# The convolution's last rows: from one turn a tile to one turn for each group of tiles

## The chip, the cores and the metric

The program runs on one core of one Trainium2 chip. The time is the device time of one execution in microseconds; of several runs the median counts. One more execution was profiled, and the profile's times are those of that execution. The granted TensorE clock was 1.00 in it throughout.

A core has five engines that work side by side, each with an instruction queue of its own that it takes strictly in order: PE (TensorE: matmuls and transposes, into PSUM banks), DVE (VectorE), ACT (ScalarE), POOL (GpSimd) and SP (SyncE, which here only issues transfers). PEld is TensorE's loading of the stationary operand. ACT issues transfers as well; while its queue does that, the instructions behind the issue wait.

## What is computed

One step of a hybrid decoder layer, for a prompt of 512 tokens and for 8 sample sequences of 8 tokens each, all in 32-bit floats. The part that matters is the causal depthwise convolution over 3072 channels (x: 2048, B: 512, C: 512), which also returns the last three rows of its input for each sequence:

```python
def causal_conv(xbc, conv_prev, conv_w, conv_b):
    L = xbc.shape[1]
    xa = jnp.concatenate([conv_prev.astype(xbc.dtype), xbc], axis=1)
    y = conv_b + sum(xa[:, j:j + L] * conv_w[j] for j in range(D_CONV))
    return jax.nn.silu(y), xa[:, L:]
```

`xbc` is a slice of `rms(h) @ W_in`. The second result goes to the outputs `conv_p` (3 rows of 3072 channels) and `conv_s` (8 sequences, 3 rows each). Around this stand a first feed-forward block, attention with a paged cache, a chunked state-space scan over 4 groups of heads that uses the convolution's result, projections, and a second feed-forward block.

## The kernel before

Activations lie transposed: channels on the 128 partitions, the 576 tokens (512 of the prompt, then 64 of the samples) along the free dimension. Matrices are multiplied in three passes: weights and activations are split into a rounded upper part and a remainder, and `mm3` (L207 to L217) adds upper by upper, upper by lower and lower by upper. It works on a half of 288 tokens at a time; for 1024 input channels a half is 8 x 3 = 24 matmuls into one PSUM bank. `acc()` hands out that bank; here it has two of them (tag "acc"). `split` (L170 to L178) makes the two parts of a weight tile: ACT the upper one (L176), DVE or, every second time, POOL the lower one (L177). Each part has four buffers, and a convolution tile takes two of each.

`conv_tile` computes one tile of 128 channels. POOL clears three columns before the prompt (L1184) and copies the samples' previous rows in (L1185); two halves of matmuls follow; DVE evicts the first (L1189), the second's prompt part (L1194) and its samples (L1196) into the tile `xr`, which is 3 + 512 + 8 x 11 columns wide. Then the last columns of `xr`, 91 of them (three of the prompt, eleven for each sample sequence), are turned on TensorE (L1202) into columns 384 to 511 of the very bank that held the second half, ACT copies the turned rows to the tile `tt` (L1204), and four transfers on ACT's queue store them: one for `conv_p` (L1205) and three for `conv_s` (L1208), one for each of the three rows. The convolution itself is one ACT instruction (L1213), three on DVE (L1215), a tanh on ACT that overwrites `xr` (L1216), and the products on DVE (L1217), ACT (L1219) and POOL (L1220).

`group_in(g)` calls `conv_tile` six times for a group: for B, for C, and for four tiles of x; there are 4 groups, so 24 tiles. `group_scan(g)` (L1295 on) is the scan of a group. Its `chunk` turns the x tiles and B with transposes (L1370, L1377, copied by ACT at L1380) and multiplies (L1386, L1390), `carry` passes the state on (L1401, L1407), and POOL scales (L1364, L1311). These small products live in banks that `sm()` hands out, two of them (tag "mm"). In the program's text the next group's `group_in` comes after a group's scan, and the scan after the `group_in` that feeds it.

The order of each engine's queue is not the order of the text. A planner simulates the time line of all engines while the program is built; it takes what is ready, the first in the text first, and what stands under `soon()` ahead of the rest. It also lets a tile of a ring (`bufs=2` and the like) wait until the readers of an earlier tile in the same buffer are done. Rings that matter here: `xr` three buffers, `tt` one, `acc` two banks, `sm()` two banks.

In time, the first group's convolutions run at 875 to 912 us, beside the end of the attention; the other groups' lie among the scan before them, at 961 to 1034, 1100 to 1142 and 1192 to 1246 us.

Of the kernel before, what the change touches and what calls it, by code (L numbers as in the profile page):

```python
# [17 lines left out]
AF = mybir.ActivationFunctionType  # L18
# [5 lines left out]
P = 128  # L24
OFFSET = 3000
D = 1024
NP = 512
NS = 64
NT = NP + NS
HT = NT // 2  # L30
B = 8
T = 8
# [3 lines left out]
CONV = 3072  # L36
# [6 lines left out]
CZ, CX, CB, CC, CDT = 0, 2048, 4096, 4608, 5120  # L43
# [46 lines left out]
def ap3(ap, offset, dims):  # L90
    return bass.AP(tensor=ap.tensor, offset=ap.offset + offset, ap=[list(d) for d in dims])


def build(ctx, tc, A, O):
    nc = tc.nc
    uid = [0]

    def tl(pool, shape, dt=F32, tag=None, bufs=None):
        uid[0] += 1
        kw = {} if bufs is None else {"bufs": bufs}  # L100
        return pool.tile(shape, dt, tag=tag, name=f"{tag}_{uid[0]}", **kw)
# [5 lines left out]
    act = nc.scalar.activation  # L107
    V = nc.vector
    G = nc.gpsimd

    constp = ctx.enter_context(pool("const"))
# [10 lines left out]
    ident = tl(constp, [P, P], tag="ident")  # L122
# [12 lines left out]
    def sm():  # L135
        return bank("mm", 2)
# [6 lines left out]
    def acc(full=False):  # L143

        wide[1] += 1
        a = wide[0]() if wide[0] and wide[1] % 2 else tl(accp, [P, 512], tag="acc")
        return a if full else a[:, :HT]
# [275 lines left out]
    with pool("h1", reuse_waits="tile") as hp:  # L423
        hts = [tl(hp, [P, NT], tag=f"h{k}") for k in range(8)]
        nrm1 = Norm(0)
        with pool("xin", side="right", reuse_waits="tile") as xi:
# [4 lines left out]
            for half in range(2):  # L431
                d = slice(half * (D // 2), (half + 1) * (D // 2))
                for c in range(5):
                    n = P if c < 4 else NS
# [5 lines left out]
            t = tr()  # L440
            nc.tensor.transpose(t[:, :8], r1, ident[:8, :8])
            V.tensor_copy(P1[:, :8], t[:, :8])
            for k in range(8):
                t = tr()
# [6 lines left out]
                t = sm()  # L451
# [5 lines left out]
            for c in range(5):  # L457
                n = P if c < 4 else NS
# [6 lines left out]
        with pool("setup2", side="right", reuse_waits="tile") as su:  # L465
            q = nc.scalar

            r1 = tl(su, [66, P], tag="r1")

            def rows(o, ap, n):  # L470
                q.dma_start(out=r1[o:o + n, :], in_=ap.rearrange("o (k p) -> (o k) p", p=P))

            rows(0, A["ffn1_norm"], 8)
            rows(8, A["mix_norm"], 8)
            rows(16, A["ffn2_norm"], 8)
            rows(24, A["ssd_norm"], 16)
            rows(40, A["conv_b"], 24)
            for i in range(2):
                q.dma_start(out=r1[64:65, i * 64:(i + 1) * 64], in_=A["q_norm"])
                q.dma_start(out=r1[65:66, i * 64:(i + 1) * 64], in_=A["k_norm"])  # L480
            t = tr()
            nc.tensor.transpose(t[:, :66], r1, ident[:66, :66])
            V.tensor_copy(P1[:, 8:], t[:, 8:66])
            V.tensor_scalar(P1[:, 40:64], t[:, 40:64], 0.5, None, ALU.mult)
            V.tensor_scalar(P1[:, 64:65], t[:, 64:65], -0.125, None, ALU.mult)
            r2 = tl(su, [96, P], tag="r2")
            q.dma_start(out=r2, in_=A["conv_w"].rearrange("o j (k p) -> (o j k) p", p=P))
            P2 = tl(constp, [P, 96], tag="P2")
            t = tr()
            nc.tensor.transpose(t[:, :96], r2, ident[:96, :96])  # L490
            V.tensor_scalar(P2, t[:, :96], 0.5, None, ALU.mult)
            r3 = tl(su, [16, 2], tag="r3")
            q.dma_start(out=r3, in_=A["d_skip"].rearrange("o (j e) -> (o j) e", e=2))
            r4 = tl(su, [16, 2, 64], tag="r4")
            V.tensor_copy(r4, r3.unsqueeze(2).to_broadcast([16, 2, 64]))
            dsk = tl(constp, [P, 16], tag="dsk")
            t = tr()
            nc.tensor.transpose(t[:, :16], r4.rearrange("j e p -> j (e p)"), ident[:16, :16])
            V.tensor_copy(dsk, t[:, :16])

            bb = tl(constp, [48, 1], tag="bb")
            behind(q.dma_start(out=bb[:32], in_=A["dt_bias"].rearrange("o h -> h o")), nrm1.insts[7])
            behind(q.dma_start(out=bb[32:48], in_=A["b_f"].rearrange("o h -> h o")), nrm1.insts[7])
            V.tensor_scalar(bb[32:48], bb[32:48], -1.0, None, ALU.mult)
            al = tl(constp, [48, 1], tag="al")
            V.memset(al, 0.0)
            behind(q.dma_start(out=al[:32], in_=A["a_log"].rearrange("o h -> h o")), nrm1.insts[7])
            act(al, al, AF.Exp)
            V.tensor_scalar(al, al, -1.0, None, ALU.mult)

            pcol = tl(su, [P, B], I32, tag="pcol")
            for b in range(B):
                q.dma_start(out=pcol[:, b:b + 1], in_=ap3(A["page_table"], b * NPG, [(1, NPG), (0, 8), (1, 1)]))
            rq = tl(su, [P, 4], tag="rq")
            q.dma_start(out=rq, in_=A["consts"][:, COFF["rq"][0]:COFF["rq"][0] + 4])
            pidx = tl(constp, [P, B, 4], I32, tag="pidx")
            pf32 = tl(su, [P, B], tag="pf32")
            V.tensor_copy(pf32, pcol)
            V.tensor_scalar(pf32, pf32, 32.0, None, ALU.mult)
            V.tensor_tensor(pidx, pf32.unsqueeze(2).to_broadcast([P, B, 4]), rq.unsqueeze(1).to_broadcast([P, B, 4]), ALU.add)  # L520
# [67 lines left out]
    win = A["w_in"][0]  # L588
# [18 lines left out]
    with pool("dtf", side="right", reuse_waits="tile") as dp:  # L607
        w = []
# [7 lines left out]
        for half in range(2):  # L616
            a = pv()
# [29 lines left out]
        for c in range(5):  # L647
            n = P if c < 4 else NS
            t = tr()
# [17 lines left out]
    with pool("att", side="right", reuse_waits="tile") as ap:  # L667
# [95 lines left out]
        for p in range(2):  # L763
            for g2 in range(0, 4, 2):
# [9 lines left out]
                for gi in range(2):  # L774
                    w = []
# [8 lines left out]
        for p in range(2):  # L784
            t = tl(mixp, [P, NT], tag="kf", bufs=2)
# [390 lines left out]

    XR = [P, 3 + NP + B * (T + 3)]

    def conv_tile(ct, w, prev, out):

        xr = tl(xz, XR, tag="xr", bufs=3)
        xsamp = xr[:, 3 + NP:]
        xsamp = xsamp.rearrange("p (b u) -> p b u", u=T + 3)
        G.memset(xr[:, :3], 0.0)  # L1184
        first = G.tensor_copy(xsamp[:, :, :3], prev.rearrange("p (j b) -> p b j", b=B))  # L1185
        a = acc()
        mm3(a, w, xs, 0)
        with soon():
            V.tensor_tensor(xr[:, 3:3 + HT], a, rbc[:, hs(0)], ALU.mult)  # L1189
        a = acc(True)  # L1190
        full, a = a, a[:, :HT]
        end = mm3(a, w, xs, 1)
        with soon():
            V.tensor_tensor(xr[:, 3 + HT:3 + NP], a[:, :NP - HT], rbc[:, HT:NP], ALU.mult)  # L1194
        with soon():
            V.tensor_tensor(xsamp[:, :, 3:], a[:, NP - HT:].rearrange("p (b t) -> p b t", t=T),  # L1196
                            rbc[:, NP:].rearrange("p (b t) -> p b t", t=T), ALU.mult)

        n = 3 + (T + 3) * B
        with soon():  # L1200
            t = full[:n, 512 - P:]
            nc.tensor.transpose(t, xr[:, NP:], ident)  # L1202
            tt = tl(xz, [n, P], tag="tt", bufs=1)
            act(tt, t, AF.Copy)  # L1204
        nc.scalar.dma_start(out=O["conv_p"][0, 0, :, ct * P:(ct + 1) * P], in_=tt[:3])  # L1205
        for j in range(3):
            r = 3 + T + j
            nc.scalar.dma_start(out=O["conv_s"][0, :, j, ct * P:(ct + 1) * P], in_=tt[r:r + (T + 3) * (B - 1) + 1:T + 3])  # L1208

        m = NP + B * (T + 3)  # L1210
        cv = tl(mixp, XR, tag="kf", bufs=2)
        wc = lambda j: P2[:, j * 24 + ct:j * 24 + ct + 1]
        act(cv[:, :m], xr[:, :m], AF.Identity, bias=P1[:, 40 + ct:41 + ct], scale=wc(0))  # L1213
        for j in range(1, 4):
            V.scalar_tensor_tensor(cv[:, :m], xr[:, j:j + m], wc(j), cv[:, :m], ALU.mult, ALU.add)  # L1215
        tanh = act(xr[:, :m], cv[:, :m], AF.Tanh)  # L1216
        last = V.scalar_tensor_tensor(out[:, :NP], xr[:, :NP], 1.0, cv[:, :NP], ALU.add, ALU.mult)  # L1217
        samples = lambda v: v[:, NP + 3:].rearrange("p (b u) -> p b u", u=T + 3)[:, :, :T]
        act(samples(xr), samples(xr), AF.Identity, bias=1.0)  # L1219
        G.tensor_tensor(out[:, NP:].rearrange("p (b t) -> p b t", t=T), samples(xr), samples(cv), ALU.mult)  # L1220
        convs.append((first, tanh, last, end))
# [3 lines left out]
    def group_in(g):  # L1225

        scT = tl(xz, [P, 6, 24], tag="scT", bufs=1)
        nc.sync.dma_start(out=scT[:, :4, :], in_=scD[:, 4 * g:4 * g + 4, :])
        nc.sync.dma_start(out=scT[:, 4:, :], in_=ap3(scD, (16 + g) * 24, [scD.ap[0], (4 * 24, 2), (1, 24)]))
        bT = tl(xz, [P, NT], tag="bT", bufs=2)  # L1230
        conv_tile(16 + g, Cols(win, CB + g * P, width=P).get(0), scT[:, 4, :], bT)
        cT = tl(xz, [P, NT], tag="cT", bufs=2)
        conv_tile(20 + g, Cols(win, CC + g * P, width=P).get(0), scT[:, 5, :], cT)
        xc = Cols(win, CX + g * 512)
        xg = tl(xz, [P, 4, NT], tag="xg", bufs=2)
        for i in range(4):
            conv_tile(4 * g + i, xc.get(i), scT[:, i, :], xg[:, i, :])
        return bT, cT, xg

    nxt = group_in(0)  # L1240
# [346 lines left out]
```

## Time and profile before

| | |
|---|---|
| median of 3 runs | 1829.32 us (1826.55 to 1835.17) |
| the profiled execution | 1829.29 us |
| its span, first to last instruction | 1827.4 us |
| turns L1202 | 24, 0.272 us each |
| copies L1204 | 24, 0.273 us each |
| transfer issues L1205, L1208 | 24 of 0.256 us, 72 of 0.651 us |

The page's first lines give each engine's busy time, its share of the span and its number of instructions. Matmuls are pipelined: one lasts 0.29 us in the trace while the next starts 0.13 us after it, so a busy share of 98% of PE does not say that it starts a matmul whenever it could. In the view of waits a row names who waited, whose end released it, the total in us, the number of times and the longest. In the timeline a row has start, duration, engine, line, operation, what is written and read, and in brackets the idle time of the engine before it with its releaser. In the rows of one line stand minimum, median and maximum in ns. A row of the windows has the stretch, its length, the busy time and number of instructions of each engine, the granted clock, the share of the DMA engines and GB/s.

### The profile page before, as it was taken

What the parts mean: (1) busy time and instruction counts of PE and PEld (TensorE: products, weight loads), DVE (VectorE), ACT (ScalarE), POOL (GpSimd) and SP (SyncE); (2) the same over time, 40 slices, a digit from 0 to 9 for tenths busy, and PEclk for the clock granted to TensorE, in tenths of its full rate; (3) what the DMA queues carried; (4) which work ended last, traced back from release to release, by engine and by line L of the source; (5) the groups of instructions that cost most, each with busy time, mean ns of one, the idle gap of its engine ahead of it and who ended that gap; (6) DMA issues with size and microseconds to landing.
All of it is one profiled execution on the core that took longest, in us unless ns stands there. A gap on an engine that the chain in (4) does not pass through costs nothing.

```text
span 1827.4 us, 38776 instructions
## 1 busy us (share of the span) xinstructions
PE 1798.5 (98%) x15315; PEld 1713.3 (94%) x15315; DVE 1014.7 (56%) x2259; ACT 758.1 (41%) x1598; POOL 630.6 (35%) x724
## 2 busy tenths in 40 slices
PE   8999999999999999999999999999999999999999
PEld 7999999999999888888998888888999999999998
DVE  4643334434426777775728857686675444444542
ACT  4333223334324565564427555555333333123322
POOL 0433002312322455453325454848452322002210
PEclk9999999999999999999999999999999999999999
DMA  5544443444546688774356554454473434543342
GB/s 164 161 120 138 129 134 109 124 137 133 120 132 197 201 243 240 244 231 158 89 164 183 153 139 112 124 151 138 153 215 93 127 116 130 152 139 110 111 124 66
DMA packets 297739, 269.72 MB, mean 148 GB/s; under 512 B 55084, under 2 KB 262108, under 8 KB 297404
## 3 DMA queue, kind: packets, MB, share of 16 engines
q1 hardware_dynamic: 229712, 184.16, 35.7%
q10 hardware_dynamic: 57844, 46.10, 8.2%
q0 software_dynamic: 10000, 36.97, 6.4%
q8 instruction: 121, 1.98, 0.5%
q14 instruction: 62, 0.51, 0.1%
HBM read 223.72 MB, written 38.73 MB: 144 GB/s over the span
## 4 chain that ended last, share of the span: by engine, by line
PE 88%; DVE 5%; DMA 3%; ACT 1%; issue 1%; POOL 1%; ACTq 0%; DVEq 0%; SPq 0%; POOLq 0%
PE acc L212 17%; PE acc L215 16%; PE acc L216 16%; PE pv L212 8%; PE pv L215 8%; PE pv L216 8%; PE tr L990 2%; PE tr L977 1%; PE mm L913 1%; PE pv L1386 1%; PE pv L944 1%; PE mm L931 1%; DVE kf L1215 1%; PE mm L1401 1%; PE pv L1028 1%
## 5 line engine op out<-in xcount | busy, mean ns | idle before, releaser
L176 ACT ACTIVATE whi<-stage 128x512 fp32r<-128x512 f32 (+2 forms) x474 | 294.3, 622 | 687.2 <-PE acc L215 589.1
L212 PE MATMUL acc<-xh,whi 128*128 128x288 f32 x1792 | 539.4, 301 | 11.1 <-DVE xr L1189 4.8
L215 PE MATMUL acc<-xl,whi 128*128 128x288 f32 x1792 | 530.4, 296 | 0.0
L216 PE MATMUL acc<-xh,wlo 128*128 128x288 f32 x1792 | 529.3, 295 | 0.0
L177 DVE TENSOR_TENSOR wlo<-stage,whi 128x512 fp32r<-128x512 f32 (+1 forms) x373 | 262.3, 703 | 257.1 <-ACT whi L176 235.0
L212 PEld LDWEIGHTS acc<-xh,whi 128*128 128x128 f32 x1792 | 336.4, 188 | 17.7 <-DVE xr L1189 7.2
L215 PEld LDWEIGHTS acc<-xl,whi 128*128 128x128 f32 x1792 | 336.6, 188 | 1.3 <-issue 1.2
L216 PEld LDWEIGHTS acc<-xh,wlo 128*128 128x128 f32 x1792 | 336.2, 188 | 0.9 <-issue 0.7
L353 POOL TENSOR_TENSOR u<-u,s 128x288 f32<-128x288 f32 x88 | 82.3, 936 | 433.9 <-DVE u L352 378.2
L177 POOL TENSOR_TENSOR wlo<-stage,whi 128x512 fp32r<-128x512 f32 (+1 forms) x101 | 133.9, 1326 | 276.3 <-ACT whi L176 243.3
L212 PE MATMUL pv<-xh,whi 128*128 128x288 f32 (+1 forms) x720 | 213.3, 297 | 0.6 <-ACT xh L227 0.6
L215 PE MATMUL pv<-xl,whi 128*128 128x288 f32 (+1 forms) x720 | 211.7, 294 | 0.0
L216 PE MATMUL pv<-xh,wlo 128*128 128x288 f32 (+1 forms) x720 | 211.6, 294 | 0.0
L212 PEld LDWEIGHTS pv<-xh,whi 128*128 128x128 f32 (+1 forms) x720 | 134.2, 186 | 1.2 <-ACT xh L227 0.8
L215 PEld LDWEIGHTS pv<-xl,whi 128*128 128x128 f32 (+1 forms) x720 | 134.1, 186 | 1.2
L216 PEld LDWEIGHTS pv<-xh,wlo 128*128 128x128 f32 (+1 forms) x720 | 134.0, 186 | 0.2
L212 PE MATMUL pv<-hh,whi 128*128 128x288 f32 x352 | 105.7, 300 | 0.0
L215 PE MATMUL acc<-hl,whi 128*128 128x288 f32 x352 | 104.1, 296 | 0.0
L212 PE MATMUL acc<-hh,whi 128*128 128x288 f32 x352 | 104.1, 296 | 0.0
L215 PE MATMUL pv<-hl,whi 128*128 128x288 f32 x352 | 104.1, 296 | 0.0
L216 PE MATMUL acc<-hh,wlo 128*128 128x288 f32 x352 | 104.1, 296 | 0.0
L216 PE MATMUL pv<-hh,wlo 128*128 128x288 f32 x352 | 103.7, 295 | 0.0
(370 smaller groups left out, 3560.1 us busy)
## 6 DMA issues: line engine op xcount, KB each, us to landing
stage<-in_w_in_dram SPq DMA_DIRECT2D x52, 512.0 KB
stage<-in_ffn_w_up_dram SPq DMA_DIRECT2D x44, 512.0 KB
stage<-in_ffn_w_gate_dram SPq DMA_DIRECT2D x43, 512.0 KB
stage<-in_ffn_w_down_dram SPq DMA_DIRECT2D x40, 512.0 KB
h<-in_state_ssm_dram SPq DMA_DIRECT2D x64, 256.0 KB
hTD<-hT ACTq DMA_DIRECT2D x32, 256.0 KB
pb<-pastD SPq DMA_DIRECT2D x32, 256.0 KB
ab<-cumD SPq DMA_DIRECT2D x32, 256.0 KB
```

The lines of the kernel that those rows point to most:

```text
L176: act(hi, view, AF.Copy)
L177: e.tensor_tensor(lo, view, hi.bitcast(F32), ALU.subtract)
L212: begin = mm(out, lhsT=hi, rhs=a, start=first and i == 0, stop=False)
L215: mm(out, lhsT=hi, rhs=b, start=False, stop=False)
L216: end = mm(out, lhsT=lo, rhs=a, start=False, stop=last and i == n - 1)
L353: G.tensor_tensor(u, u, sil[half], ALU.mult)
L913: mm(s[:, :n], lhsT=q, rhs=ks[2 * self.p + e][:, :n], start=hl == 0, stop=hl == 1)
L931: nc.tensor.transpose(t[:, j * P:(j + 1) * P], lt[:, j * P:(j + 1) * P], ident)
L944: mm(self.ob[o:o + 32, i * P:(i + 1) * P], lhsT=vtok[j][:, v0:v0 + 32], rhs=self.pts[e][:, j * P:(j + 1) * P], start=j == 0, stop=j == i)
L977: nc.tensor.transpose(t[:, i * P:(i + 1) * P], kk[:, i, p * P:(p + 1) * P], ident)
L990: mm(s[kv * 32:(kv + 1) * 32, :], lhsT=self.q(kv), rhs=self.kT[kv // 2], start=True, stop=True)
L1028: mm(ob[kv * 32:(kv + 1) * 32, :64], lhsT=self.pt[:, i * P + kv * 32:i * P + (kv + 1) * 32], rhs=vv[:, i, kv * 64:(kv + 1) * 64], start=jq ...
```

## The change

The last rows are no longer turned tile by tile. A tile `tail` of 27 columns for each convolution tile gathers them: POOL copies the three last columns of the prompt and the 8 x 3 last columns of the samples out of `xr` (two copies a tile, under `soon()`). Columns are ordered so that after the turn the prompt's rows of all tiles come first and the samples' after them. `store3`, called once for B and C together and once for the four x tiles, turns the whole of it in a bank of `sm()`, copies it once on ACT and stores it with two transfers on ACT's queue. These are 8 turns, 8 copies and 16 transfers in place of 24, 24 and 96, and 48 new copies on POOL. `tail` and `tt` have one buffer each. `store3` is not under `soon()`. Besides, two constants of one column each, `bb` and `al`, become the columns of one tile.

```diff
-            bb = tl(constp, [48, 1], tag="bb")
+            ba = tl(constp, [48, 2], tag="ba")
+            bb, al = ba[:, :1], ba[:, 1:]
...
-            al = tl(constp, [48, 1], tag="al")
...
+    def rows3(n):
+
+        return tl(xz, [P, 108], tag="tail", bufs=1)[:, :27 * n]
+
+    def store3(tail, n, ct, step):
+
+        t = sm()
+        nc.tensor.transpose(t[:27 * n, :P], tail, ident)
+        tt = tl(xz, [108, P], tag="tt", bufs=1)
+        act(tt[:27 * n], t[:27 * n, :P], AF.Copy)
+        for name, r0, rows in (("conv_p", 0, 3), ("conv_s", 3 * n, 24)):
+            nc.scalar.dma_start(out=ap3(O[name], ct * P, [(step * P, n), (CONV, rows), (1, P)]), in_=tt[r0:r0 + rows * n])
+
-    def conv_tile(ct, w, prev, out):
+    def conv_tile(ct, w, prev, out, last3):
...
-        a = acc(True)
-        full, a = a, a[:, :HT]
+        a = acc()
...
-        n = 3 + (T + 3) * B
+        tail, i, n = last3
         with soon():
-            t = full[:n, 512 - P:]
-            nc.tensor.transpose(t, xr[:, NP:], ident)
-            tt = tl(xz, [n, P], tag="tt", bufs=1)
-            act(tt, t, AF.Copy)
-        nc.scalar.dma_start(out=O["conv_p"][0, 0, :, ct * P:(ct + 1) * P], in_=tt[:3])
-        for j in range(3):
-            r = 3 + T + j
-            nc.scalar.dma_start(out=O["conv_s"][0, :, j, ct * P:(ct + 1) * P], in_=tt[r:r + (T + 3) * (B - 1) + 1:T + 3])
+            G.tensor_copy(tail[:, 3 * i:3 * i + 3], xr[:, NP:NP + 3])
+            G.tensor_copy(tail[:, 3 * n + 24 * i:3 * n + 24 * (i + 1)].rearrange("p (b j) -> p b j", j=3), xsamp[:, :, T:])
...
+        tail = rows3(2)
-        conv_tile(16 + g, Cols(win, CB + g * P, width=P).get(0), scT[:, 4, :], bT)
+        conv_tile(16 + g, Cols(win, CB + g * P, width=P).get(0), scT[:, 4, :], bT, (tail, 0, 2))
...
-        conv_tile(20 + g, Cols(win, CC + g * P, width=P).get(0), scT[:, 5, :], cT)
+        conv_tile(20 + g, Cols(win, CC + g * P, width=P).get(0), scT[:, 5, :], cT, (tail, 1, 2))
+        store3(tail, 2, 16 + g, 4)
...
+        tail = rows3(4)
         for i in range(4):
-            conv_tile(4 * g + i, xc.get(i), scT[:, i, :], xg[:, i, :])
+            conv_tile(4 * g + i, xc.get(i), scT[:, i, :], xg[:, i, :], (tail, i, 4))
+        store3(tail, 4, 4 * g, 1)
```

## The prediction

> **What bounds the kernel now.** I read the page first, for the engines and the chain that ended last.
>
> ```profile
> span 1827.4 us, 38776 instructions
> PE 1798.5 (98%) x15315; PEld 1713.3 (94%) x15315; DVE 1014.7 (56%) x2259; ACT 758.1 (41%) x1598; POOL 630.6 (35%) x724
> PE 88%; DVE 5%; DMA 3%; ACT 1%; issue 1%; POOL 1%; ACTq 0%; DVEq 0%; SPq 0%; POOLq 0%
> ```
>
> TensorE bounds it: whatever leaves ScalarE's queue or the DMA queues is worth nothing unless TensorE waited for it. So the next view is the windows of the four stretches in which the 24 convolution tiles run; after the length stand the busy times of PE, PEld, DVE, ACT and POOL, then clock, DMA share and GB/s.
>
> ```profile
> 875.00:912.00 37.00, 35.30 (x256) 33.49 (x254) 32.57 (x53) 20.73 (x40) 14.55 (x23) 1.00 0.34 75
> 912.00:961.00 49.00, 48.98 (x371) 48.96 (x371) 14.94 (x27) 10.96 (x18) 10.39 (x14) 1.00 0.60 161
> 961.00:1034.00 73.00, 68.33 (x585) 60.40 (x584) 62.92 (x136) 52.82 (x144) 41.70 (x50) 1.00 0.66 186
> 1100.00:1142.00 42.00, 39.82 (x288) 37.55 (x287) 35.14 (x78) 21.32 (x44) 19.97 (x27) 1.00 0.39 107
> 1192.00:1246.00 54.00, 50.94 (x390) 48.43 (x390) 45.62 (x95) 27.42 (x60) 28.05 (x35) 1.00 0.48 144
> ```
>
> The second row is the attention projection, for comparison: there TensorE is dense. In the four others it is idle for 1.7, 4.7, 2.2 and 3.1 us. The clock is at 1.00 throughout, so only waits and work can change. The view of waits, restricted to TensorE from 866 to 1246 us, says who ended them (total, times, longest):
>
> ```profile
> PE acc L212 <- DVE xr L1189: 4.8, 8, 2.2
> PE acc L212 <- ACT tt L1204: 3.7, 8, 1.4
> PE tr L1348 <- POOL cT L1220: 1.4, 2, 0.7
> PE acc L212 <- ACT wdec L1291: 0.6, 1, 0.6
> ```
>
> The first two are the convolution's own. The timeline shows the mechanism at its first tile:
>
> ```profile
> 874.80 0.29 PE L215 MATMUL acc<-xl,whi 128*128 128x288 f32 x1
> 874.93 0.29 PE L216 MATMUL acc<-xh,wlo 128*128 128x288 f32 x1
> 875.06 0.27 PE L1202 MATMUL acc<-ident,xr 128*91 128x128 f32 x1
> 875.26 0.46 DVE L1189 TENSOR_TENSOR xr<-acc,rbc 128x288 f32<-128x288 f32 x1 [2.68 <-PE acc L216]
> 875.37 0.27 ACT L1204 ACTIVATE tt<-acc 91x128 f32<-91x128 f32 x1
> 875.77 0.40 PE L212 MATMUL acc<-xh,whi 128*128 128x288 f32 x1 [0.44 <-DVE xr L1189]
> 876.01 0.29 PE L215 MATMUL acc<-xl,whi 128*128 128x288 f32 x1
> ```
>
> There are two accumulator banks. One was just filled by a half (24 matmuls, 0.13 us apart) and must be evicted by L1189. The other holds the half before; it was evicted long ago, but the turn L1202 still writes into it and L1204 still reads it. So after each such pair of halves TensorE finds no free bank: from 875.06 to 876.01 are 0.95 us for two steps that in the dense stream take 0.26.
>
> **The change part by part.**
>
> *The wait for a bank.* With the turn out of the accumulator, that bank is free once the tile's two evictions L1194 and L1196 are done, which a whole half of 24 x 0.13 = 3.1 us follows. Of the 16 waits the view counts 4.8 + 3.7 = 8.5 us. It begins to count only where the last matmul's modelled 0.29 us end, though the next could start after 0.13: 16 x (0.29 - 0.13) = 2.6 us more. The first matmul after a wait is followed 0.24 us later (875.77 to 876.01), not 0.13: 16 x 0.11 = 1.8 us. A check at the first tile: 0.44 + 0.14 + 0.11 = 0.69 = 0.95 - 0.26. Together 8.5 + 2.6 + 1.8 = 12.9 us. Would something else be late in their place? The longest one says:
>
> ```profile
> 1009.84 1.02 PE L1401 MATMUL mm<-xde,bt 128*128 128x512 f32 x2
> 1010.81 1.84 DVE L1215 SCALAR_TENSOR_TENSOR kf<-xr,P,kf 128x600 f32<-128x600 f32 x1
> 1012.58 0.45 DVE L1189 TENSOR_TENSOR xr<-acc,rbc 128x288 f32<-128x288 f32 x1
> 1013.07 0.40 PE L212 MATMUL acc<-xh,whi 128*128 128x288 f32 x1 [2.21 <-DVE xr L1189]
> ```
>
> Here VectorE is the late one. With the other bank free the half starts near 1010.9, and the bank that L1189 frees at 1013.0 is wanted only 3.1 us later, at 1014.0. It goes too, but with 1 us to spare.
>
> *The turns.* 24 go and 8 come. Eight transposes in a row take 0.99 us (chain in order of time), so a slot is 0.12 us: 24 x 0.12 - 8 x 0.12 = 1.9 us less. That the eight new ones turn 54 or 108 columns and not 91 doesn't change the moving side, which stays 128.
>
> ```profile
> 600.24 0.99 PE tr L990 x8
> L1204 ACT ACTIVATE tt<-acc x24: 251/273/275, 875.4 to 1233.2; 91x128 f32<-91x128 f32 x24
> L1205 ACTq DMA_DIRECT2D out_dram<-tt x24: 255/256/413, 875.7 to 1233.5; - x24
> L1208 ACTq DMA_DIRECT2D out_dram<-tt x72: 645/651/759, 876.0 to 1235.3; - x72
> ```
>
> *ScalarE and its queue.* 16 of 24 copies go (16 x 0.273 = 4.4 us), and 96 issues (72 x 0.651 + 24 x 0.256 = 53.0 us) become 16. The issue of a transfer of 96 rows in three dimensions is not in the trace. By the 8-row one it is 0.65 us; if it grew with the rows, 0.651 x 96/8 = 7.8 us. I take 0.65, since the transfer of 128 partitions by 4 blocks below costs 0.40. So ScalarE's queue has 43 us less by this, and at the other end 8 x 7.8 + 8 x 1 = 70 us, 17 more than now. On the path I count either as nothing: apart from L1204, the view of waits has one wait of TensorE for ScalarE, the 0.6 us of L1291. What covers it are the four buffers of weights' upper halves (L176), two a tile: they are made a tile ahead, and without that TensorE would wait for each.
>
> ```profile
> L1452 ACTq DMA_DIRECT2D out_dram<-x x4: 395/400/404, 1019.6 to 1286.8; - x4
> L1185 POOL COPY xr<-scT x24: 206/216/821, 873.5 to 1220.3; 128x24 f32<-128x24 f32 x24
> L1215 DVE SCALAR_TENSOR_TENSOR kf<-xr,P,kf x72: 794/844/1934, 875.6 to 1235.8; 128x600 f32<-128x600 f32 x72
> L1364 POOL TENSOR_TENSOR ab<-ab,cT x24: 1270/1292/1587, 980.7 to 1270.2; 128x512 f32<-128x512 f32 x24
> ```
>
> *POOL.* 48 copies come. The 24 of 128x24 have a twin, L1185, 0.216 us; the 24 of 128x3 I put at no more than that: 24 x 2 x 0.216 = 10.4 us. POOL is busy 14.55 of 37, 41.70 of 73, 19.97 of 42 and 28.05 of 54 us, so its idle time holds them. They add a wait: each stands in POOL's queue until VectorE's L1196, and for the first tile of the next gather until the one `tail` buffer has been turned. Behind it stand L177 (weights' lower halves), L1364 of the scan and L1220. The tanh L1216, which overwrites xr, must wait for both copies; three L1215 of 0.844 us lie between the eviction and it, 2.5 us of cover.
>
> *The new turn's own wait.* TensorE now waits for POOL eight times where L1202 followed VectorE 24 times. Of TensorE's weight loads, the view of waits has one for that:
>
> ```profile
> PEld acc L1202 <- DVE xr L1196: 0.2, 1, 0.2
> ```
>
> The nearest wait for POOL is L1348 <- POOL cT: of four C tiles two waited, 1.4 us in all, so eight turns at that rate cost 2.8 us; I take 2.0, between the two rows and nearer to POOL's. Behind the waiting turn stands all of TensorE's queue. Ends: 0 and one POOL instruction ahead of each pair of copies, 8 x (1.29 + 0.43) = 13.8 us.
>
> *VectorE under POOL's copies.* L1215 has a median of 0.844 and a longest of 1.934 us. If each new copy holds up a VectorE instruction for its own 0.216 us, that is 10.4 us of VectorE; nothing of it at the other end. I take 1.0 us on the path, for the reasons under the second rival.
>
> *bb and al in one tile.* Same loads and operations, in setup while the first feed-forward runs dense on TensorE: nothing.
>
> Sum: -12.9 - 1.9 + 2.0 + 1.0 = -11.8 us. The profiled execution took 1829.3 us, as good as the median of the runs (1829.32): 1829.3 - 11.8 = 1817.5 us.
>
> **The rivals.**
>
> *VectorE takes over and half is given back: 1824.* In the first convolution stretch VectorE is busy 32.57 of 37 us. TensorE's need falls by a quarter of 14.8, to 33.3 us; VectorE's rises by 12 copies x 0.216 = 2.6 to 35.2. It would then end 1.9 us after TensorE, in four groups 7.6 us. 1829.3 - 12.9 - 1.9 + 2.0 + 7.6 = 1824.1. For it: the 2.21 us wait above, where VectorE was late. Against it: evictions are put ahead of the rest in its queue, and 912 to 961 us leaves it 34 us to catch up, so I count about an eighth. The Trainium skill has a rule for this ("SBUF — State Buffer", section "Who interferes with whom"): a VectorE instruction with two SBUF inputs and a GpSimd instruction that reads SBUF lock each other out for the whole instruction. The 1.934 us of an L1215 agree with it; by it all 48 copies count, and 1824 would be the result.
>
> *ScalarE's relief counts after all: 1810.* In 961 to 1034 us ScalarE is busy 52.82 of 73 us and issues 6 tiles x 2.2 = 13 us of these transfers. If its products come earlier in the scans, another 2 us per group fall: 1817.5 - 8 = 1809.5. Against it: next to no wait of TensorE there names ScalarE.
>
> *POOL stands in the way: 1840, slower.* The place is the turn at the head of TensorE's queue. From the second group on the bank of small products is in the hands of the scan before:
>
> ```profile
> 993.91 0.21 DVE L1196 TENSOR_TENSOR xr<-acc,rbc 128x64 f32<-128x64 f32 x1
> 1008.48 0.25 ACT L1380 ACTIVATE bt<-mm 128x128 f32<-128x128 f32 x1
> ```
>
> The rows of the next tile are there at 993.9, the bank of the turn before it perhaps only at 1008.7. If POOL's queue stands on such a copy, the scan's L1364 and the weights stand behind it and TensorE waits for them. It decides from 14.8/8 = 1.9 us per turn; one POOL instruction of 1.29 us, the two copies and another such one make 3.0 us, 8 x 3.0 = 24: 1829.3 - 14.8 + 24 = 1838.5, a little over with VectorE's 1.0. For it: 41.70 of 73 us of POOL are busy there. Against it: L1202 waited for VectorE once, so the planned order leaves slack between an eviction and its turn, and the planner sees these waits.
>
> *Nothing happens.* If the accumulator banks were late for another reason, only the turns' slots would go: 1827. The 0.05 us between L1189's end (875.72) and TensorE's restart (875.77) speak against it.
>
> **How the numbers follow.** About 0.5% (9 us) is what a measurement of this kernel can tell from no change. Forecast (1813 to 1821) 0.50; half given back or nothing (1821 to 1829) 0.28; larger gain (1806 to 1813) 0.10; slower (1830 to 1842) 0.12. Faster by over 0.5% means under 1820.2: the larger gain and nine tenths of the forecast, 0.55. Slower by over 0.5% is over 1838.5: most of its case, 0.08. Within: 0.37. The range from 1808 to 1831 leaves out some 0.03 below and 0.10 above; it holds the ends of the unknown costs one at a time: both at nothing 1814.5, POOL's 13.8 us 1829.3, VectorE's 10.4 us 1826.9.
>
> **What would show it.** Right: no wait of a convolution half for L1189 or for the copy of the turned rows, TensorE idle under 1 us in the first stretch, 8 turns, 16 transfers on ScalarE's queue. Wrong: a turn, or L177 and L1364, waiting for POOL's new copies by over 1 us each; L1215's median well over 0.844; or halves that now wait for L1196. What would make it wrong beyond these: the planner orders the queues anew, and waits far from the convolution may come or go.

## The result and the profile after

| | before | after |
|---|---|---|
| median of 20 runs | 1832.62 us (1826.55 to 1836.88) | 1835.79 us (1833.97 to 1842.26) |
| ratio to before | | 1.0021, 95% interval 1.0013 to 1.0029 |
| the profiled execution | 1829.29 us | 1835.63 us |
| granted clock in it | 1.000 | 0.995 |

The change makes the kernel 3 to 4 us slower, a small loss that the interval separates from none. The time lies above the range of the forecast, 1808 to 1831, and nothing of its gain of 12 us is to be seen. Of the 6.3 us between the two profiled executions about half is real; the other half is that the one of before lies 3 us under its median.

The page of the kernel after, the same three lines as before:

```profile
span 1833.8 us, 38719 instructions
PE 1801.9 (98%) x15299; PEld 1715.7 (94%) x15299; DVE 1019.4 (56%) x2259; ACT 756.6 (41%) x1582; POOL 648.2 (35%) x772
PE 39%; DVE 2%; ACT 1%; DMA 1%; issue 1%; POOL 0%; ACTq 0%; SPq 0%; POOLq 0%
```

The counts are those of the change: 16 fewer turns on PE and copies on ACT, 48 more copies on POOL. (The shares of the chain aren't to be compared: it could be followed back through less than half of the span here.) In this kernel the evictions of the convolution are L1202, L1206 and L1208, the gathering copies L1213 and L1214, the turn L1186, its copy L1188 and the transfers L1190; what was L1215, L1370, L1377, L1477 is now L1221, L1380, L1387, L1487.

Where in the program is the time lost? The last transposition of the last normalization, in the rows of line L277, is the mark. First the kernel before, then the kernel after:

```profile
L277 DVE STREAM_TRANSPOSE rbc<-rsy x1: 778/778/778, 1400.9 to 1400.9; 128x576 f32<-128x576 f32 x1
```

```profile
L277 DVE STREAM_TRANSPOSE rbc<-rsy x1: 778/778/778, 1407.7 to 1407.7; 128x576 f32<-128x576 f32 x1
```

6.8 us are lost by then, and 0.4 us won from there to the end (426.5 us before, 426.1 after). The second feed-forward is not touched. So we look at the windows of the convolution stretches, after:

```profile
875.00:912.00 37.00, 36.13 (x272) 35.68 (x271) 33.72 (x53) 20.75 (x36) 22.58 (x38) 1.00 0.33 78
961.00:1034.00 73.00, 68.34 (x594) 60.72 (x593) 64.75 (x137) 54.26 (x144) 50.55 (x62) 1.00 0.64 183
1100.00:1142.00 42.00, 37.37 (x280) 35.26 (x278) 37.25 (x72) 19.23 (x39) 21.31 (x41) 0.98 0.32 94
1192.00:1246.00 54.00, 48.91 (x345) 45.45 (x344) 43.79 (x91) 25.26 (x52) 19.05 (x38) 0.91 0.39 116
```

In the first stretch TensorE's idle time fell from 1.7 to 0.9 us, and 16 more matmuls were started: that is a gain of the kind that was forecast. In the last two it rose, from 2.2 to 4.6 and from 3.1 to 5.1 us, and the clock, 1.00 throughout before, is 0.98 and 0.91 there. The view of TensorE's waits, 866 to 1246 us, after:

```profile
PE acc L212 <- DVE xr L1208: 3.3, 3, 1.8
PE mm L1380 <- POOL xg L1226: 2.2, 1, 2.2
PE tr L1445 <- DVE dk L1371: 1.9, 1, 1.9
PE mm L1186 <- POOL tail L1214: 1.7, 2, 1.4
PE mm L1380 <- DVE cbm L1346: 1.4, 1, 1.4
```

The 8.5 us for L1189 and L1204 are gone. The new turn's wait for POOL is 1.7 us in all. New are waits of the scan's transposes (L1380, L1445), which had none before. The timeline of TensorE at the end of the third group's convolution, after, shows how they come about:

```profile
1135.38 0.29 PE L216 MATMUL acc<-ygh,wlo 128*128 128x288 f32 x1
1135.51 0.27 PE L1186 MATMUL mm<-ident,tail 128*108 128x128 f32 x1
1135.62 0.33 PE L268 MATMUL mm<-ssq,cst 128*128 128x64 f32 x2
1136.81 0.52 PE L1380 MATMUL mm<-ident,xg 128*64 128x128 f32 x3 [0.86 <-DVE ssq L273]
1137.17 0.27 PE L1387 MATMUL mm<-ident,bT 128*64 128x128 f32 x1
1139.65 0.92 PE L1380 MATMUL mm<-ident,xg 128*64 128x128 f32 x5 [2.21 <-POOL xg L1226]
1140.73 1.12 PE L1396 MATMUL pv<-dk,xdt 64*64 64x64 f32 x16 [0.15 <-DVE xdt L1383]
...
1145.10 2.08 PE L1411 MATMUL mm<-xde,bt 128*128 128x512 f32 x2
...
1148.82 0.40 PE L212 MATMUL acc<-ygh,whi 128*128 128x288 f32 x1
```

From 1135.51 to 1148.82 us not one matmul into an accumulator bank starts; TensorE has only the scan's products and transposes. The two accumulator banks hold the first two halves of the group's output product (`ygh`), and these can't be evicted: the eviction L1487 multiplies by the group normalization's factor, and that factor has only now been started. L268 is the second product of this normalization (the sum of squares for the samples' tokens). It stands directly behind the turn L1186. The rows of VectorE show the rest of the chain, after:

```profile
1136.52 0.24 DVE L273 STREAM_TRANSPOSE ssq<-mm 128x64 f32<-128x64 f32 x1
1147.05 0.78 DVE L277 STREAM_TRANSPOSE ssq<-rsy 128x576 f32<-128x576 f32 x1
1148.32 0.81 DVE L1487 TENSOR_TENSOR u<-acc,ssq 128x288 f32<-128x288 f32 x2
```

Between the first two rows lies a reciprocal root in many small steps that take turns with other work. The same product and the same first eviction in the kernel before:

```profile
1109.54 0.33 PE L268 MATMUL mm<-ssq,cst 128*128 128x64 f32 x2
...
1121.83 0.77 DVE L277 STREAM_TRANSPOSE ssq<-rsy 128x576 f32<-128x576 f32 x1
...
1140.91 0.46 DVE L1477 TENSOR_TENSOR u<-acc,ssq 128x288 f32<-128x288 f32 x1 [0.46 <-PE acc L216]
```

L268 ran 26.1 us earlier, in the midst of the convolution, and the factor was there 18 us before it was first used. In the last group L268 moved by 33 us, from 1202.79 to 1236.01. The windows at the ends of these two convolutions, first before, then after:

```profile
1135.00:1149.00 14.00, 13.63 (x102) 13.10 (x102) 10.41 (x19) 5.76 (x11) 10.09 (x15) 1.00 0.25 78
1233.00:1247.00 14.00, 13.75 (x120) 12.97 (x119) 12.12 (x22) 6.58 (x18) 10.54 (x11) 1.00 0.48 136
```

```profile
1135.00:1149.00 14.00, 10.00 (x76) 6.67 (x75) 13.78 (x38) 9.34 (x28) 5.83 (x10) 0.76 0.35 103
1237.00:1251.00 14.00, 11.20 (x88) 8.16 (x86) 13.01 (x39) 9.86 (x28) 4.82 (x6) 0.76 0.43 124
```

TensorE is idle 4.0 and 2.8 us where it was idle 0.4 and 0.3, and a mean clock of 0.76 over 14 us is 0.24 x 14 / 0.5 = 6.7 us at half clock in each.

Why does L268 stand behind the turn? Both take a bank from `sm()`, which has two and hands them out in the order of the program's text. That order is (shortened, with comments added):

```python
gated = group_scan(g, *cur)
...
nxt = group_in(g + 1)      # ends with store3(tail, 4, ...): t = sm()
...
group_out(g, *gated)       # begins with rowscale: t2 = sm(), the product L268
...                        # the next group_scan begins with chunk(4, None): t = sm()
```

A planner may move instructions, but a bank of a ring goes to its users in turn. The turn of the x tiles needs the last of them to be convolved and gathered; until then it holds its place in the ring, and neither L268, which needs no result of this convolution (the program only orders it behind the C tile's matmuls), nor the transposes of the next scan (L1380, L1387), each of which needs one tile of it, can run. The old turns sat in the accumulator's own bank and held no place in this ring.

That is theory T1, the **bank order**. Its rivals: T2, the **copies on POOL** hold up VectorE, or what stands behind them in POOL's queue; T3, the **gain was never there**, the waits for the accumulator being covered by something else; and T4, **replanning**: the planner lays all queues anew, and any other order may be faster or slower by chance.

### The profile page after: what moved, and what is told of

Its sections match the earlier page's. It is cut to its first block, busy times and chain, and to the rows that moved or that the text cites. A ratio compares the mean times of both kernels' runs of the same rounds, so it can differ in the third digit from the quotient of the medians.

```text
span 1833.8 us, 38719 instructions
## 1 busy us (share of the span) xinstructions
PE 1801.9 (98%) x15299; PEld 1715.7 (94%) x15299; DVE 1019.4 (56%) x2259; ACT 756.6 (41%) x1582; POOL 648.2 (35%) x772
## 5 line engine op out<-in xcount | busy, mean ns | idle before, releaser
L177 DVE TENSOR_TENSOR wlo<-stage,whi 128x512 fp32r<-128x512 f32 (+1 forms) x373 | 263.9, 708 | 257.1 <-ACT whi L176 248.3
L177 POOL TENSOR_TENSOR wlo<-stage,whi 128x512 fp32r<-128x512 f32 (+1 forms) x101 | 134.4, 1331 | 213.9 <-ACT whi L176 195.5
```

Source lines behind the costliest of these rows:

```text
L177: e.tensor_tensor(lo, view, hi.bitcast(F32), ALU.subtract)
```

## The experiments

Each ratio is to the kernel before on the same chip in the same rounds. e1 to e4 ran together (before: 1832.75 us), e5 to e8 (1835.09), and e10 and e11 (1835.20).

| | this median, us | ratio | 95% interval |
|---|---|---|---|
| after | 1835.79 | 1.0021 | 1.0013 to 1.0029 |
| e1, the turn after the chunk | 1822.89 | 0.9949 | 0.9934 to 0.9965 |
| e2, the turn after the norm | 1824.49 | 0.9949 | 0.9935 to 0.9963 |
| e3, the turn in the accumulator | 1825.99 | 0.9958 | 0.9943 to 0.9974 |
| e4, before, x turns in `sm()` | 1851.59 | 1.0101 | 1.0084 to 1.0117 |
| e5, before, with POOL's copies | 1843.23 | 1.0045 | 1.0032 to 1.0058 |
| e6, the norm's product in another ring | 1828.46 | 0.9959 | 0.9944 to 0.9974 |
| e7, both turns late | 1821.98 | 0.9936 | 0.9921 to 0.9951 |
| e8, before, no last rows | 1823.06 | 0.9933 | 0.9921 to 0.9946 |
| e10, before, norm in another ring | 1834.01 | 0.9996 | 0.9987 to 1.0005 |
| e11, e7 with e6 | 1824.57 | 0.9944 | 0.9932 to 0.9956 |

**e1 and e2: only the place in the text.** The x tiles' `store3` is called later: in e1 after the next scan's first chunk, and so behind L268 and behind that chunk's transposes; in e2 behind L268 but ahead of the chunk. The instructions are the same.

```diff
-        store3(tail, 4, 4 * g, 1)
-        return bT, cT, xg
+        return bT, cT, xg, tail
...
-        def group_scan(g, bT, cT, xg):
+        def group_scan(g, bT, cT, xg, tail):
...
             chunk(4, None)
+            store3(tail, 4, 4 * g, 1)
```

(e2 has the added line ahead of `chunk(4, None)`.)

> The changed kernel, with the turn of the four x tiles written in the text behind the next scan's first chunk, so that the group norm's second product (L268) and that chunk's transposes get their banks of small products ahead of it. Bank theory: the transposes spread among the convolution's matmuls again, TensorE has output matmuls to fill with, its clock stays at 1.00, and the time is 4 to 10 us under the kernel before (about 1822 to 1828). POOL theory (the 48 copies and the wait for them cost the time): nothing changes, 2 to 5 us over the kernel before, as the changed kernel. Replanning theory (any other order falls out by chance): anywhere, with no tie to where L268 stands.

> The same turn one step earlier in the text: behind the group norm, but still ahead of the first chunk's transposes. Bank theory: tells the two waiters apart. If L268 (and with it all evictions of the output matmuls) is what counts, it is within 2 us of e1_turn_after_chunk; if the chunk's transposes count, it is within 2 us of the changed kernel. I expect the first, 1824 to 1830. POOL theory: as the changed kernel, 2 to 5 us over the kernel before.

Both took 0.9949 of before: a loss of 0.21% became a gain of 0.51% through the place of one call. The timeline of e1 at the same product:

```profile
1113.56 0.29 PE L1186 MATMUL mm<-ident,tail 128*54 128x128 f32 x1 [1.38 <-POOL tail L1214]
1113.69 0.33 PE L268 MATMUL mm<-ssq,cst 128*128 128x64 f32 x2
```

L268 is back from 1135.62 to 1113.69, and now stands directly behind the turn of B and C, which it still follows in the text. That TensorE waits 1.38 us for POOL there stayed, so at this turn T2's price is the same in the slow kernel and in the fast one. e1 and e2 can't be told apart: what the chunk's transposes lose beside L268 is too small to be seen here.

**e3: the turn back in the accumulator.** Gathering and `store3` stay, but the turn goes into the end of the last tile's accumulator bank, as in the kernel before, and it and its copy stand under `soon()`, as there.

```diff
-        t = sm()
-        nc.tensor.transpose(t[:27 * n, :P], tail, ident)
+        t = full[:, 512 - P:]
+        with soon():
+            nc.tensor.transpose(t[:27 * n, :P], tail, ident)
...
-        act(tt[:27 * n], t[:27 * n, :P], AF.Copy)
+        with soon():
+            act(tt[:27 * n], t[:27 * n, :P], AF.Copy)
...
-        a = acc()
+        a = acc(True)
+        full, a = a, a[:, :HT]
...
+        return full
```

> The changed kernel with its eight turns in the spare columns of the last tile's accumulator bank, as the kernel before did it 24 times; POOL's gather stays. Bank theory: the banks of small products are as before, no delay of L268, clock 1.00; eight waits of about 0.7 to 1.5 us for the accumulator stay of the 16, so 1 to 7 us under the kernel before (about 1825 to 1831). POOL theory: 2 us or more over the kernel before.

0.9958: the loss is gone too, though all 48 copies are there. Its waits, TensorE from 866 to 1246 us, have the accumulator's price again, on a third of the turns:

```profile
PE acc L1187 <- POOL tail L1217: 2.1, 5, 0.7
PE acc L212 <- ACT tt L1190: 1.5, 3, 0.6
```

**e4: the bank alone, put into the kernel before.** Every fourth x tile's turn takes a bank of `sm()`; nothing else differs, and POOL gathers nothing.

```diff
-            t = full[:n, 512 - P:]
+            t = sm()[:n, :P] if ct < 16 and ct % 4 == 3 else full[:n, 512 - P:]
```

> The kernel before with one part of the change alone: only the fourth x tile of each group is turned in a bank of small products, the other 20 tiles as before, no gather on POOL. Bank theory: L268 and the first chunk's transposes queue behind that turn, TensorE starves after the convolution and its clock falls below 1.00; 3 to 12 us over the kernel before. POOL theory: as the kernel before, within 2 us.

1.0101, or 18.8 us: the direction of T1, and over its upper end by half. Behind the turn the picture of the kernel after comes back, with a mean clock of 0.76 over the 14 us from 1147 and from 1249. The timeline of e4:

```profile
1146.93 0.27 PE L1202 MATMUL mm<-ident,xr 128*91 128x128 f32 x1
1147.04 0.33 PE L268 MATMUL mm<-ssq,cst 128*128 128x64 f32 x2
```

L268 comes 37.5 us later than in before and 11.4 later than in after. It follows the group's last turn, which was 5.2 us earlier in after than in before and is 6.2 us later here. But not all of the 18.8 us is the bank's. The first row of the view of waits, and one of the eight in the timeline:

```profile
PE acc L212 <- ACT tt L1204: 10.3, 8, 3.9
```

```profile
1110.72 0.61 PE L212 MATMUL acc<-xh,whi 128*128 128x288 f32 x1 [3.85 <-ACT tt L1204]
```

The wait for L1204 has grown from 3.7 to 10.3 us, by two waits of 3.85 us, here and at 1212.12, where no L268 is concerned: ScalarE's queue has L1313, which waits 3.0 and 4.6 us for POOL, ahead of the copy L1204, which came ahead of it in before. Behind each the granted clock is near half (0.52 from 1108.5 to 1115 and from 1211 to 1217 us). That is another order of ScalarE's queue, so T4. So e4 shows the direction of T1 and not its price.

**e5: the copies alone, put into the kernel before.** The tile's rows are gathered by POOL into a tile that nobody reads; turns, copies and transfers stay.

```diff
+        tail = tl(xz, [P, 27], tag="tail", bufs=1)
...
+            G.tensor_copy(tail[:, :3], xr[:, NP:NP + 3])
+            G.tensor_copy(tail[:, 3:].rearrange("p (b j) -> p b j", j=3), xsamp[:, :, T:])
```

> The kernel before, with POOL's 48 gathering copies added and their result read by nobody: the price of POOL's part alone. Bank theory: under 2 us on either side of the kernel before. POOL theory (copies that hold up VectorE and stand in POOL's queue cost the time): 3 us or more over it, and L1215 longer than its 0.844 us.

A miss: 1.0045, or 8.1 us, where the bank theory had under 2. So in this order adding the copies costs time. The rows of the first copy and of the convolution's products:

```profile
L1202 POOL COPY tail<-xr x24: 179/644/798, 875.0 to 1238.8; 128x3 f32<-128x3 f32 x24
L1218 DVE SCALAR_TENSOR_TENSOR kf<-xr,P,kf x72: 795/844/1939, 877.1 to 1242.6; 128x600 f32<-128x600 f32 x72
```

It isn't the one that the prediction had in mind: the convolution's products have the same median as before, 0.844 us; it is POOL's small copy that is held up, 0.644 us in the median for three columns. (The Trainium skill, "SBUF — State Buffer", section "Who interferes with whom", says that a VectorE instruction with two SBUF inputs and a GpSimd instruction that reads SBUF lock each other out. The 0.644 us against a shortest of 0.179 agree, with the wait on POOL's side.) The view of waits (TensorE, 866 to 1300 us) begins:

```profile
PE acc L212 <- DVE xr L1189: 4.4, 6, 2.3
PE acc L212 <- DVE u L1480: 4.2, 2, 2.1
PE acc L212 <- ACT tt L1207: 4.2, 9, 1.2
```

The first and the third are about those of before (4.8 and 3.7 us). New are the two of 2.1 us for L1480, the output's eviction. The timeline of VectorE shows what made the first of them late:

```profile
1168.91 4.73 DVE L177 TENSOR_TENSOR wlo<-stage,whi 128x512 fp32r<-128x512 f32 x1
1174.17 0.81 DVE L1480 TENSOR_TENSOR u<-acc,ssq 128x288 f32<-128x288 f32 x2
```

L177, the last but one ahead of it, took 4.73 us where its median is 0.692, while POOL ran one instruction behind the other from 1168.13 to 1173.09 us. The second is the same, at 1264.16. So here VectorE is held up, and not by a gathering copy: none runs there. Behind both waits the clock is at 0.50 (1176 to 1178 and 1272 to 1274 us). e7, which makes the same copies, has one such L177 (4.71 us) and one such wait; before and after have none. So part of e5's loss comes from the order in which the planner laid the queues, T4; how much the copies themselves cost wasn't settled.

**e6: the norm's product in another ring.** In the kernel after, L268 takes its bank from `pv()`, the ring of the scan's products; `store3` stays where it was.

```diff
-            t2 = sm()
+            t2 = sm() if first is None else pv()
```

> The changed kernel with one tile moved: the group norm's second product (L268) takes a bank of the ring pv in place of one of sm(), so it stands behind no turn; the turn of the x tiles stays where it is, and the first chunk's transposes stay behind it. If L268 alone makes the loss: 5 to 10 us under the kernel before, as e1 and e2, and clock at 0.998 or more. If the chunk's transposes count as well: between the changed kernel and e2.

0.9959. The timeline of e6:

```profile
1113.75 0.33 PE L268 MATMUL pv<-ssq,cst 128*128 128x64 f32 x2
1114.89 0.27 PE L1186 MATMUL mm<-ident,tail 128*54 128x128 f32 x1
```

L268 now runs ahead of even the turn of B and C. One bank for one product turns +0.21% into -0.41%; of the 0.85% between after and the best version (e7) this is 0.62, near three quarters. A piece of the rest stands in the first row of e6's view of waits (TensorE, 866 to 1300 us):

```profile
PE pv L268 <- POOL ssq L1325: 4.9, 1, 4.9
```

This is the L268 of 1028.73. The sum of squares that it needs stood in POOL's queue behind a copy of 24 columns (L1198) that took 3.19 us, with a median of 0.396; the clock is at 0.50 behind it (1028 to 1032 us). e2 has this wait too, e7 one of 1.7 us. So T2, as a queue on POOL that makes others late, is not absent from the fast kernels either.

**e7: both turns late.** As e1, and the turn of B and C is moved behind the chunk as well; each kind of `tail` gets its own buffer.

```diff
-        return tl(xz, [P, 108], tag="tail", bufs=1)[:, :27 * n]
+        return tl(xz, [P, 27 * n], tag=f"tail{n}", bufs=1)
...
-        store3(tail, 2, 16 + g, 4)
...
             chunk(4, None)
+            store3(tbc, 2, 16 + g, 4)
+            store3(tail, 4, 4 * g, 1)
```

> As e1_turn_after_chunk, and the turn of B and C goes behind the next scan's first chunk too (with a tail of its own), so that no turn stands ahead of L268. Bank theory: as e1 or a little better, 8 to 13 us under the kernel before, since in e1 the turn of B and C came before L268 and cost one wait of 1.4 us. A loss against e1 would speak for chance in the replanning.

0.9936, the lowest of all that compute the whole output. Its window at the end of the third group's convolution, its view of waits (TensorE, 866 to 1300 us), and the mark from above:

```profile
1135.00:1149.00 14.00, 14.00 (x122) 13.10 (x122) 12.16 (x24) 7.62 (x20) 10.81 (x15) 1.00 0.30 82
```

```profile
PE acc L212 <- DVE u L1487: 2.1, 1, 2.1
PE mm L268 <- POOL ssq L1323: 1.7, 1, 1.7
...
PE acc L212 <- DVE xr L1208: 0.9, 1, 0.9
```

```profile
L277 DVE STREAM_TRANSPOSE rbc<-rsy x1: 779/779/779, 1394.0 to 1394.0; 128x576 f32<-128x576 f32 x1
```

In the 14 us TensorE starts 122 matmuls where it started 76 in after, at full clock, and the mark is passed 13.7 us earlier than in after.

**e8: what there is to gain.** The kernel before without its last rows: the turn, the copy and the four transfers of each tile are left out, and the outputs `conv_p` and `conv_s` are not written.

```diff
-        n = 3 + (T + 3) * B
-        with soon():
-            t = full[:n, 512 - P:]
...
-            nc.scalar.dma_start(out=O["conv_s"][0, :, j, ct * P:(ct + 1) * P], in_=tt[r:r + (T + 3) * (B - 1) + 1:T + 3])
```

> The kernel before without the convolution's last rows: no turn, copy or transfer, and outputs conv_p and conv_s are not written. It measures the two gains that the forecast counted, 12.9 us of waits for a bank and 24 turns at 0.12 us (2.9 us): 16 us under the kernel before if they were sized right; about 8 to 10 us if part of those waits comes back elsewhere.

0.9933, or 12.0 us, between the two values that were expected. T3 falls: the old way of storing the rows does cost 12 us. And e7's 0.9936 is the same within the intervals, so in e7's order the new way costs nothing that can be measured, its 48 copies and 8 turns with it.

**e10 and e11: controls.** e10 is e6's edit in the kernel before, e11 is e6's edit in e7.

> Control for e6: the kernel before with the same one tile moved (L268 into a bank of pv), nothing of the change. Bank theory: L268 waited for no turn there, so nothing is to be gained: within 3 us of the kernel before. If the move gains 5 us or more here too, what e6 gained was not the change's own loss.

> Both remedies at once: both turns behind the next scan's first chunk, and L268 in a bank of pv. Bank theory: one remedy takes the delay away already, so as e7, 10 to 15 us under the kernel before, with nothing added by the second. If it falls clearly under e7, something else waits in the ring of small products.

0.9996 and 0.9944: where no late turn stands ahead of L268 in the ring, moving it to another ring brings nothing. So e6's gain isn't a gain of the other ring as such.

T1 is shown as the main cause. How far L268 starts behind the norm's first product (L266, for the prompt's tokens) can be read in every trace: in the stretches of 1100 and of 1192 us it is 32.7 and 34.7 us in after, 30.8 and 31.2 in e4, and at most 7.6 in all the others. The four edits that free L268 from the turn (e1, e2, e3, e6) each take away 0.6 to 0.7%, though e6 moves one tile and nothing else, and where it is free, freeing it does nothing (e10, e11). By T4 alone four edits would hardly gain the same. But T4 has a size of its own: e5 loses 0.45% with L268 at most 3.3 us behind, and part of e4's loss lies elsewhere.

## Why the prediction was wrong, step by step

- **The wait for a bank** was read rightly, and as a gain it was too large. The waits for L1189 and L1204 are gone in after. But e8, which also has no new turns to pay, gains 12.0 us (0.54 to 0.79% of 1835, so 10 to 14.5), where the steps gave 12.9 for the waits and 24 x 0.12 = 2.9 for the turns, 15.8. Which of the three parts of the 12.9 was too large wasn't tried, nor whether other waits took their place: e8's profiled execution, 3.6 us over its median, has 10.5 us of TensorE's waits from 866 to 1246 us where before has 11.5, the longest 2.8 us for a copy on ScalarE (L1369). One new wait for a late eviction has come: L1208, 3.3 us in three times, in after.
- **The turns:** 8 for 24, as said.
- **ScalarE and its queue:** the issue of 96 rows, an estimate of 0.65 us, took 0.67 in after (L1190). That the 42 us which left the queue (53.0 less 16 x 0.67) were counted at nothing agrees with e8: its whole gain is no more than waits and slots.
- **The new turn's own wait**, taken at 2.0 us, was 1.7 us in after. As a wait of the turn for POOL this was right. The step failed in what it left unasked, and this is why the forecast missed. It said "Behind the waiting turn stands all of TensorE's queue" and priced the turn's lateness on TensorE's queue alone. The planner does keep the turn out of TensorE's way until its rows are there. But what waits for the turn is the next user of its bank. The rival *POOL stands in the way* even quoted the ring of small products, and asked only whom the turn waits for in it (the scan before), not who comes behind the turn: L268 and the next chunk. L268 came 26 and 33 us late, the output's evictions waited for it, and TensorE had nothing to fill with. So neither the sum nor a rival had the 0.85% of the time, some 16 us, by which after differs from e7.
- **VectorE under POOL's copies**, 1.0 us between 0 and 10.4: it can't be measured in e7's order, and e5, with the copies in before's order, lost 8.1 us, a part of it where no copy runs. The bounds held both; the price hangs on the order around the copies. VectorE did not take over: the median of the products is unchanged.
- **The rivals:** "nothing happens" is refuted by e8. "POOL stands in the way" had the right sign but another cause. "ScalarE's relief" is nowhere to be seen.
- The sum itself, -11.8 us, was forecast for the kernel after and missed it. That e7 measures the same (-0.64%, 11.7 us; 13.1 us by the medians) is luck, two errors that cancel: a gain 3.8 us too large, and 4.0 us (1.0 + 2.0 + 1.0) for the new turns, their wait and the copies, which together cost nothing there that can be measured. It is no evidence for the sum's terms.
- **Among the signs** named beforehand came one turn that waited over 1 us for POOL (1.38), the halves that wait for L1196, now L1208, and the reordering of the queues; the latter stood in one half of a sentence, without a place or a price.

## What to carry to other kernels

When an operation gets its buffer from a ring that is handed out in program order, list the ring's next users in the text, not only the last ones: whatever the new user waits for, they wait for as well, however early their own inputs are there. An instruction that nobody needs soon (here a store of rows that no later step reads) belongs behind those that others need; moving its call in the text by one function cost nothing and was worth 0.7% here. And a gain read off a view of waits can be right at its place and be lost elsewhere, so check who is released by each event that the change makes later.

## What the runs showed of the hardware

The granted clock fell to half in three episodes of the kernel after, where the kernel before held 1.00. A window in the midst of one, after:

```profile
1141.00:1147.00 6.00, 6.00 (x52) 3.78 (x51) 5.97 (x19) 5.53 (x17) 1.28 (x2) 0.50 0.38 96
```

TensorE is busy throughout at 0.50: the two L1411 of 1145.10 take 2.08 us, where two of the same line took 1.02 at 1009.84 in before. The idle gaps ahead of it were 0.86 and 2.21 us. The Trainium skill, "TensorE: Matmul & The Clock Gate", section "Part 1: The HAM clock gate (the "warmup" mystery)", has the clock fall to half after an idle window of about 3.4 us; none of these gaps is that long. The same page of the Trainium skill, section "Part 4: PE-mode transpose", says that a transpose doesn't count as busy the same way. If L1380 and L1387, which are transposes, are counted as idle, 4.8 us lie between the end of L268 (1135.95) and L1396 (1140.73), and then the trace agrees for this episode. It does not for the one at 1222.4 to 1225.8 us, which follows a single gap of 1.80 us; what runs just ahead of that gap are matmuls of the scan and no transposes:

```profile
1219.15 0.60 PE L1358 MATMUL tr<-cT,bT 128*128 128x128 f32 x4
1221.56 0.37 PE L212 MATMUL acc<-xh,whi 128*128 128x288 f32 x1 [1.80 <-DVE xr L1208]
```

Nor does the length of a gap alone decide: behind one of 2.21 us at 1013.07 in before the clock stayed at 1.00, behind one of 2.27 us at 1015.31 in e5 it fell to half. What does decide stays open here. How much of the loss is the half clock and how much the missing work wasn't tried: no run held the clock up with the banks in the wrong order.

A copy of three columns on POOL, which the prediction put at no more than 0.216 us, had a median of 0.188 us and a longest of 1.469 in after, and a median of 0.644 in e5: the same instruction is three times as long in another order of the queues. The other side of it is the L177 on VectorE in e5, 4.73 us in place of 0.692, beside a POOL queue without a gap.
